# Small unused gaps between the large on-chip arrays of a two-layer decoder trunk

## The chip, the cores and the metric

The kernel runs on one core of a Trainium2 chip. The metric is the device time of one execution in microseconds (us); the median of several executions is compared. One core has five engines that run their own instruction streams and wait for one another by semaphores: TensorE (PE, matrix products), VectorE (DVE), ScalarE (ACT), GpSimd (POOL) and SyncE (SP). The profile shows the loads of TensorE's stationary operand as an engine of its own (PEld). Arrays lie in the on-chip memory SBUF, which has 128 partitions; an address below is the byte offset in a partition, the same for all of them.

## The reference

A batch of one sequence of 256 positions and width 2048 goes through two layers, all in float32:

```python
h = x
for layer in range(2):
    hn = rms_norm(h, norm_mix[layer])
    if layer % 2 == 0:
        mix = recurrent_mixers(hn, ...)     # one projection 2048 -> 6144, RG-LRU and HGRN2 heads, 2048 -> 2048
    else:
        mix = dilated_attention(hn, positions, w_qkv, w_o)   # 16 heads, 2048 -> 6144, 2048 -> 2048
    h = h + mix
    h = h + squared_relu_mlp(rms_norm(h, norm_mlp[layer]), mlp_w1[layer], mlp_w2[layer])  # 2048 -> 8192 -> 2048
return rms_norm(h, final_norm)
```

Nearly all of the work is in the seven large weight matrices.

## The kernel before

**Products in parts.** A float32 product is made of float32r matmuls (a type that TensorE takes at one column per step, with fewer bits). Each weight tile `raw` of 128 x 2048 is split into `hi` (ScalarE, a cast, L112) and `lo` = raw - hi (VectorE, L113). The activations are split likewise into a high and a low half that lie beside each other in `bufa` and `bufb` (16 blocks of 2 x 256 columns each). Of the four partial products three are computed: high x hi, high x lo, low x hi.

**Two forms.** In `direct` (L230), used by the input projections of layer 0, the weight part is the stationary operand (128 columns of `hi` or `lo`) and 256 columns of `bufa` or `bufb` are streamed. In `tokens` and in `times` inside `blocks`, used everywhere else, an activation slice of 128 columns is stationary and 512 columns of `hi` or `lo` are streamed. Every matmul has another stationary operand than the one before it, or loads the same one anew, so one weight load stands between any two matmuls. They all go through the helper `mm` (L196), which also fixes their order on TensorE.

**Seven products for eight.** `blocks` multiplies 2 x 2 blocks with seven products. The sums of activation blocks that this needs are kept, split, in `formx` (in the pool `both`) and `formh` (in the pools `pair0`, `forms1`); they are stationary operands too. Sums of weight blocks are formed in `s` and `t`, by VectorE and by DMAs that add on their way, and split like `raw`.

**What sets the order.** The loads of weights (SP's queue, some on POOL's) are issued in the order of a list of units, a few units ahead of their use. A scheduler places the instructions on each engine by priorities; small pieces of other work (transposes, attention heads, normalizations) are put off by a counter and slipped in between groups of twelve large matmuls.

**Where the arrays lie.** Pools take their addresses one behind the other, in the order in which they are opened, and a tile's place follows from the sizes ahead of it, rounded up to 32 bytes. First come the constants (`cst`), then `act` with `xall` and `bufa`, then `wraw`, `whi`, `wlo` with three tiles of 8 KB each, `tmp` with small tiles, `acts` with `bufb`, and behind it either the pools of layer 0's mixers or `both`, `pair0` and their successors. All large tiles are multiples of 512 bytes. In the built program before, `bufa` starts at 23328, `raw` at 56096, `hi` at 80672, `lo` at 105248, `bufb` at 132384, `formx` at 165152 and `formh` at 197920: each is 288 modulo 512. Every slice that a matmul reads of them starts a multiple of 512 bytes further on (128 columns of 4 bytes, or 256, or 512). `qk` and `st`, small tiles of layer 0's HGRN2 heads, lie at 416 modulo 512.

Of the kernel before, what the change touches and what calls it, by code (L numbers as in the profile page):

```python
# [10 lines left out]
F32 = mybir.dt.float32  # L11
# [9 lines left out]
P = 128  # L21
# [21 lines left out]
def trunk_kernel(ctx, tc, begin, xtok, cols, tab, masks, pos, fin, w_in, w_gate, w_out, w_qkv, w_o, w1, w2, out):  # L43
# [3 lines left out]
    act = pool("act")  # L47
# [3 lines left out]
    tmp = pool("tmp", 2)  # L51
# [8 lines left out]
    xall = act.tile([P, KB * S], F32, name="xall")  # L60
    xres = xall.rearrange("p (j d) -> p j d", j=2)
    bufa = act.tile([P, KB, 2 * S], F32R, name="bufa")

    units = []
    made = {}
# [138 lines left out]
    def put_off(wait, *fs):  # L204
        later.extend((clock[0] + wait, f) for f in fs)
# [369 lines left out]
    pairs, turned_ = ExitStack(), ExitStack()  # L575

    def open_pairs(layer):
        pool_ = pairs.enter_context(tc.tile_pool(name=f"pair{layer}", bufs=1))
        return pool_, pool_.tile([P, 4, 2, 512], F32R, name="formh")

    def part_forms(f, k, m, at, src):
# [8 lines left out]
        V.tensor_tensor(s4, a12, s2, OP.add)  # L590

    both = ctx.enter_context(tc.tile_pool(name="both", bufs=1))
    formx = both.tile([P, 4, 2, 512], F32R, name="formx")
    pair, formh = open_pairs(0)


# [6 lines left out]
    late = []  # L603
# [48 lines left out]
    def pair_forms(forms, k, src, z):  # L652
        h, l = (src[:, k:k + 2, c * S:c * S + S].bitcast(F32) for c in range(2))
        V.tensor_tensor(z.rearrange("p i j c -> p i (j c)"), h, l, OP.add)
        a11, a21, a12, a22 = (z[:, i, j] for i in range(2) for j in range(2))
        combos(a22, a11, a21, a12, a11, a21, a12, a22)
        part_forms(forms, k % 8 // 2, 1, slice(0, 4), z.rearrange("p i j (one c) -> p one (i j) c", one=1))
# [260 lines left out]
    def token_pair(i, c0, ready, raw=()):  # L918
        spare_ = wk.tile([P, 512], F32, name="q0", bufs=1) if not c0 and ATTENTION[:i].count("q") % 2 else None

        def out_(n, j):
            return xres[:, j, c0 + 512 * n:c0 + 512 * n + 512] if spare_ is None or (n, j) != (0, 0) else spare_

        def put(n, j, r=rt):
            def event(bank):
                with urgent():
                    if (n, j) in raw:
                        A.copy(out_(n, j), bank)
                    else:
                        A.activation(out_(n, j), bank, AF.Copy, scale=r[:, j:j + 1])  # L930
            return event

        def add(n, j, bank, r=rt):
            o = out_(n, j)
            with urgent():
                if (n, j) in raw:
                    V.tensor_tensor(o, bank, o, OP.subtract)
                else:
                    V.scalar_tensor_tensor(o, bank, r[:, j:j + 1], o, op0=OP.mult, op1=OP.add)

        def whole(n, j):
            if (n, j) in raw:
                with urgent():
                    A.activation(out_(n, j), out_(n, j), AF.Copy, scale=rt[:, j:j + 1])
            ready(n, j, out_(n, j))

        def final(n, j, bank):
            if (n, j) != (1, 0):
                put(n, j)(bank)
            else:  # L950
                add(n, j, bank)
            if (n, j) != (1, 1):
                whole(n, j)

        def u3(bank):
            add(1, 1, bank, rtn)
            whole(1, 1)

        blocks(w_qkv, 8 * i, 0, feature, formx,
               {"t2": put(1, 0, rtn), "t3": u3}, final)  # L960

    def queries_keys(i, raw=()):
        turned = [wk.tile([P, 4, S], F32, name="qT", bufs=1), wk.tile([P, 4, S], F32, name="kT", bufs=1)]

        def ready(n, j, o):
            t = o.rearrange("p (h c) -> p h c", h=4)
            r = t[:, :, :32].rearrange("p h (two c) -> p h two c", two=2)
            per = lambda a: a[:, j][:, None, :].to_broadcast([P, 4, 16])
            with urgent():
                b = wk.tile([P, 4, 2, 16], F32, name="rb", bufs=2)  # L970
                c = wk.tile([P, 4, 2, 16], F32, name="rc", bufs=2)
                V.tensor_tensor(b[:, :, 0], r[:, :, 1], per(sinT[:, 0]), OP.mult)
                V.tensor_tensor(b[:, :, 1], r[:, :, 0], per(sinT[:, 1]), OP.mult)
                V.tensor_tensor(c, r, cosT[:, j][:, None, None, :].to_broadcast([P, 4, 2, 16]), OP.mult)
                V.tensor_tensor(r, c, b, OP.add)

            def turns():
                p = psc.tile([P, 4, P], F32, name="pl", bufs=2)
                for h in range(4):
                    turn(p[:, h], t[:, h])  # L980
                with urgent():
                    A.copy(turned[n][:, :, j * P:j * P + P], p)

            put_off(WAIT_Q, turns)

        token_pair(i, 0, ready, raw)
        return turned

    def head(hd, q, k, wait):
        def scores():  # L990
            ps_ = psc.tile([P, 384], F32, name="pl", bufs=2)
            mm(ps_[:, :P], q[:, :P], k[:, :P], start=True, stop=True)
            mm(ps_[:, P:], q[:, P:], k, start=True, stop=True)
            s = wk.tile([P, 384], F32, name="as", bufs=3)
            nm = wk.tile([P, 2], F32, name="nm", bufs=3)
            ll = wk.tile([P, 2], F32, name="ll", bufs=3)
            with urgent():
                for j, sl in enumerate((slice(0, P), slice(P, 384))):
                    V.tensor_tensor_reduce(s[:, sl], ps_[:, sl], lnc[:, sl], -P ** -0.5, 3e38, OP.add, OP.min,
                                           nm[:, j:j + 1])  # L1000
                    lut(s[:, sl], s[:, sl], AF.Exp, bias=nm[:, j:j + 1], scale=-1.0, accum_out=ll[:, j:j + 1])
                V.reciprocal(ll, ll)
                for j, sl in enumerate((slice(0, P), slice(P, 384))):
                    A.activation(s[:, sl], s[:, sl], AF.Copy, scale=ll[:, j:j + 1])
            put_off(wait, lambda: turned(s))

        def turned(s):
            pt = psc.tile([P, 384], F32, name="pd", bufs=1)
            for j in range(3):
                turn(pt[:, j * P:j * P + P], s[:, j * P:j * P + P])  # L1010
            st = wkt.tile([P, 384], F32, name="pT", bufs=8)
            with urgent():
                A.copy(st, pt)
            ready_[hd] = st

        return scores

    def mix(hd, st):
        vs = slice(D // 2 + (hd % 8) * P, D // 2 + (hd % 8) * P + P)
        po = psc.tile([P, S], F32, name="pd" if hd % 2 else "po", bufs=1)  # L1020
        mm(po, xres[:, 0, vs], st[:, :S], start=True, stop=False, skip_group_check=True)
        mm(po[:, P:], xres[:, 1, vs], st[:, S:], start=False, stop=True, skip_group_check=True)
        z = tmp.tile([P, S], F32, name="z")
        with urgent():
            A.copy(z, po)
        split_to(mixed(hd), z)
# [3 lines left out]
    for i, what in enumerate(ATTENTION):  # L1030
        if what == "v":
            token_pair(i, D // 2, lambda *_: None)
            if hd == 16:
                assert len(ready_) == 8
                mixers.close()
                late.append(pairs.enter_context(tc.tile_pool(name="forms1", bufs=1)).tile(
                    [P, 8, 512], F32R, name="formh"))
            put_off(2, *(lambda h=h: mix(h, ready_.pop(h)) for h in range(hd - 8, hd)))
            if hd == 8:
                put_off(EARLY, *(lambda k=k: pair_forms(early_forms, k, bufb, wk.tile(  # L1040
                    [P, 512], F32, name="q0", bufs=1).rearrange("p (i j c) -> p i j c", i=2, j=2))
                    for k in range(0, 8, 2)))
        else:
            q, k = queries_keys(i, ((1, 0),) if not i else ())
            for h in range(4):
                put_off(WAIT_Q + 1 + 2 * h, head(hd, q[:, h], k[:, h], WAIT_S))
                hd += 1
# [141 lines left out]
```

## Time and profile before

| what | value |
|---|---|
| median of 3 runs | 2132.87 us (2132.70 to 2132.93) |
| profiled execution | 2133.06 us, span of the instructions 2131.3 us |
| granted TensorE clock, mean | 0.999 |
| busy share of the span | TensorE 100%, weight loads 84%, VectorE 84%, ScalarE 65%, GpSimd 3% |
| data moved by DMA | 488.71 MB, 229 GB/s mean |

A row of the chain in order of time has the start in us, the length in us, the engine, the tile written, the line of the kernel and the number of instructions. A row of the timeline has the start, the time from the first start to the last end, the engine, line and operation, the output and the inputs (streamed operand first, stationary second) with shapes, and how many equal instructions follow each other. Matmuls are pipelined: an end lies behind the next one's start, so the distance between starts is what counts. In the rows of groups stand the busy time, the mean of one in ns, and the idle time ahead of them with what ended it.

### The profile page before, as it was taken

What the parts mean: (1) busy time and instruction counts of PE and PEld (TensorE: products, weight loads), DVE (VectorE), ACT (ScalarE), POOL (GpSimd) and SP (SyncE); (2) the same over time, 40 slices, a digit from 0 to 9 for tenths busy, and PEclk for the clock granted to TensorE, in tenths of its full rate; (3) what the DMA queues carried; (4) which work ended last, traced back from release to release, by engine and by line L of the source; (5) the groups of instructions that cost most, each with busy time, mean ns of one, the idle gap of its engine ahead of it and who ended that gap; (6) DMA issues with size and microseconds to landing.
All of it is one profiled execution on the core that took longest, in us unless ns stands there. A gap on an engine that the chain in (4) does not pass through costs nothing.

```text
span 2131.3 us, 26730 instructions
## 1 busy us (share of the span) xinstructions
PE 2120.9 (100%) x10542; PEld 1797.6 (84%) x10542; DVE 1788.8 (84%) x1962; ACT 1378.2 (65%) x1543; POOL 66.8 (3%) x85
## 2 busy tenths in 40 slices
PE   9999999999999999999999999999999999999998
PEld 8989998888888888888888888888888888888886
DVE  7777888888888888888988797788897888888887
ACT  7445565776476567567666777776756765755764
POOL 0000000000000000000000000000000000000000
PEclk9999999999999999999999999999999999999999
DMA  8444446686777677677887767777767768777773
GB/s 336 162 162 158 161 148 224 206 269 233 227 237 253 230 240 253 227 241 231 270 279 218 241 199 247 254 247 228 246 237 253 236 212 269 238 234 227 271 225 146
DMA packets 69806, 488.71 MB, mean 229 GB/s; under 512 B 7808, under 2 KB 8320, under 8 KB 11952
## 3 DMA queue, kind: packets, MB, share of 16 engines
q1 hardware_dynamic: 58176, 410.96, 51.1%
q0 software_dynamic: 11216, 75.70, 18.3%
q8 instruction: 82, 1.34, 0.3%
q14 instruction: 44, 0.36, 0.0%
q10 hardware_dynamic: 288, 0.34, 0.0%
HBM read 482.78 MB, written 4.19 MB: 228 GB/s over the span
## 4 chain that ended last, share of the span: by engine, by line
PE 99%; DVE 0%; ACT 0%; DMA 0%; issue 0%; ACTq 0%; DVEq 0%; POOLq 0%
PE p L196 62%; PE po L196 14%; PE pd L196 13%; PE pt L196 5%; PE pl L199 2%; PE pl L470 1%; PE pl L196 0%; PE pd L199 0%; DMA ppi<-in_pos 0%; PE pd L454 0%; DVE lo L113 0%; ACT hi L112 0%; PE pl L465 0%; PE po L495 0%; PE po L496 0%
## 5 line engine op out<-in xcount | busy, mean ns | idle before, releaser
L113 DVE TENSOR_TENSOR lo<-raw,hi 128x2048 fp32r<-128x2048 f32 (+2 forms) x397 | 787.1, 1991 | 164.5 <-ACT hi L112 159.4
L112 ACT CAST hi<-raw 128x2048 fp32r<-128x2048 f32 (+2 forms) x397 | 657.3, 1671 | 335.1 <-PE p L196 175.5
L196 PE MATMUL p<-hi,bufa 128*128 128x512 f32 x1488 | 482.0, 394 | 0.0
L196 PE MATMUL p<-hi,bufb 128*128 128x512 f32 x1128 | 363.1, 391 | 0.0
L196 PEld LDWEIGHTS p<-hi,bufa 128*128 128x128 f32 x1488 | 279.2, 188 | 57.3 <-DVE bufa L245 0.5
L113 DVE TENSOR_TENSOR lo<-s,hi 128x2048 fp32r<-128x2048 f32 (+1 forms) x164 | 285.9, 1753 | 28.6 <-ACT hi L112 27.6
L112 ACT CAST hi<-s 128x2048 fp32r<-128x2048 f32 (+1 forms) x164 | 242.7, 1480 | 98.2 <-DVE s L164 54.2
L196 PE MATMUL p<-lo,bufa 128*128 128x512 f32 x744 | 287.6, 390 | 0.2 <-DVE lo L113 0.2
L196 PEld LDWEIGHTS p<-hi,bufb 128*128 128x128 f32 x1128 | 211.7, 188 | 43.7
L196 PE MATMUL p<-lo,bufb 128*128 128x512 f32 x564 | 219.5, 389 | 0.0
L196 PE MATMUL p<-bufa,hi 128*128 128x256 f32 x1024 | 193.2, 287 | 0.0
L196 PEld LDWEIGHTS p<-lo,bufa 128*128 128x128 f32 x744 | 139.9, 188 | 28.0 <-DVE lo L113 0.7
L196 PEld LDWEIGHTS p<-bufa,hi 128*128 128x128 f32 x1024 | 161.2, 191 | 0.2
L196 PE MATMUL p<-bufa,lo 128*128 128x256 f32 x512 | 146.5, 286 | 0.0
L112 ACT CAST hi<-t 128x2048 fp32r<-128x2048 f32 x41 | 78.5, 1914 | 99.6 <-PE p L196 91.1
L113 DVE TENSOR_TENSOR lo<-t,hi 128x2048 fp32r<-128x2048 f32 x41 | 94.0, 2292 | 55.4 <-ACT hi L112 55.0
L196 PEld LDWEIGHTS p<-lo,bufb 128*128 128x128 f32 x564 | 105.9, 188 | 21.5
L196 PE MATMUL p<-hi,formh 128*128 128x512 f32 x368 | 120.7, 391 | 0.0
L196 PE MATMUL p<-hi,formx 128*128 128x512 f32 x352 | 115.9, 390 | 0.0
L196 PE MATMUL po<-hi,bufb 128*128 128x512 f32 x320 | 103.7, 390 | 0.0
L196 PEld LDWEIGHTS p<-bufa,lo 128*128 128x128 f32 x512 | 98.0, 191 | 0.0
L164 DVE TENSOR_TENSOR s<-s,raw 128x1024 f32<-128x1024 f32 x82 | 96.4, 1216 | 0.1
(319 smaller groups left out, 3292.4 us busy)
## 6 DMA issues: line engine op xcount, KB each, us to landing
raw<-in_w SPq DMA_DIRECT2D x224, 1024.0 KB, 6.1
raw<-in_w_in SPq DMA_DIRECT2D x44, 1024.0 KB, 4.8
raw<-in_w_qkv SPq DMA_DIRECT2D x42, 1024.0 KB, 6.9
t<-in_w SPq DMA_DIRECT2D x32, 1024.0 KB, 4.9
t<-in_w POOLq DMA_DIRECT2D x32, 1024.0 KB, 8.7
s<-in_w POOLq DMA_DIRECT2D x17, 1024.0 KB, 8.4
raw<-in_w_out SPq DMA_DIRECT2D x15, 1024.0 KB, 4.8
raw<-in_w_o SPq DMA_DIRECT2D x14, 1024.0 KB, 7.7
```

The source lines that it names most:

```text
L112: a = A.copy(h, w)
L113: v = V.tensor_tensor(l, w, h.bitcast(F32), OP.subtract)
L164: V.tensor_tensor(s, s, held["c"][:, at:at + 1024], OP.add)
L196: chain[:] = [after(T.matmul(*args, **kw), chain)]
L199: chain[:] = [after(T.transpose(out_, in_, ident), chain)]
L470: T.matmul(pl[:, j], kq[:, js], halves(qp[:, js], c, True), start=True, stop=True)
```

## The change

Five tiles are allocated that nothing reads or writes. They lie at the end of `act`, in `tmp`, and at the start of `both`, `pair0` and `forms1`, and push what follows by 64 or 128 bytes.

```diff
     bufa = act.tile([P, KB, 2 * S], F32R, name="bufa")
+    act.tile([P, 16], F32, name="gap0", bufs=1)
+    tmp.tile([P, 32], F32, name="gap1", bufs=1)
...
     def open_pairs(layer):
         pool_ = pairs.enter_context(tc.tile_pool(name=f"pair{layer}", bufs=1))
+        pool_.tile([P, 16], F32, name="gap3", bufs=1)
         return pool_, pool_.tile([P, 4, 2, 512], F32R, name="formh")
...
     both = ctx.enter_context(tc.tile_pool(name="both", bufs=1))
+    both.tile([P, 16], F32, name="gap2", bufs=1)
     formx = both.tile([P, 4, 2, 512], F32R, name="formx")
...
-                late.append(pairs.enter_context(tc.tile_pool(name="forms1", bufs=1)).tile(
+                forms1 = pairs.enter_context(tc.tile_pool(name="forms1", bufs=1))
+                forms1.tile([P, 16], F32, name="gap4", bufs=1)
+                late.append(forms1.tile(
                     [P, 8, 512], F32R, name="formh"))
```

In the built program the offsets modulo 512 become:

| array | before | after |
|---|---|---|
| `bufa` | 288 | 288 |
| `raw`, `hi`, `lo` | 288 | 352 |
| `bufb` | 288 | 480 |
| `formx` | 288 | 32 |
| `t`, `s` | 288 | 32 |
| `formh` (both pools) | 288 | 96 |
| `qk`, `st` | 416 | 96 |

## The prediction

> **What bounds the kernel now.** I read the page's first two parts, then the chain of work, then that chain in order of time, and last the timeline of single matmuls, since the change can only touch what one instruction costs.
>
> ```profile
> span 2131.3 us, 26730 instructions
> PE 2120.9 (100%) x10542; PEld 1797.6 (84%) x10542; DVE 1788.8 (84%) x1962; ACT 1378.2 (65%) x1543; POOL 66.8 (3%) x85
> PEclk9999999999999999999999999999999999999999
> ...
> PE 99%; DVE 0%; ACT 0%; DMA 0%; issue 0%; ACTq 0%; DVEq 0%; POOLq 0%
> ```
>
> TensorE is busy for the whole span at the full granted clock, and 99% of the chain that ends last is TensorE. So the time is a sum over matmuls of the distance from one start to the next. That distance is steady. The chain in order of time (start, length, what):
>
> ```profile
> 217.18 6.72 PE p L196 x56
> 592.87 13.60 PE p L196 x60
> ```
>
> The first row is a run of 256-column float32r matmuls in the input projections: 6.72 / 56 = 120.0 ns each. The other is a run of 512-column ones: 13.60 / 60 = 226.7 ns each. 256 more columns cost 106.7 ns, so one column costs 0.417 ns and each matmul pays a further 13.3 ns whatever its width (226.7 - 512 x 0.417). The built program has 7,956 float32r matmuls of 512 columns and 1,632 of 256: 7,956 x 0.2267 = 1,803 us and 1,632 x 0.120 = 196 us, together 1,999 of the 2,131.3 us.
>
> What does the stationary operand do meanwhile? From the timeline of an MLP stretch (start, duration, engine):
>
> ```profile
> 1000.05 0.39 PE L196 MATMUL po<-lo,bufa 128*128 128x512 f32 x1
> ...
> 1000.73 0.39 PE L196 MATMUL po<-lo,bufa 128*128 128x512 f32 x1
> 1000.73 0.41 PEld L196 LDWEIGHTS po<-hi,bufa 128*128 128x128 f32 x2
> ```
>
> The next weight load starts in the same 10 ns in which a matmul starts (both 1000.73). So while 512 columns of one array are streamed, 128 columns of another are read, from the same instant on, at a fixed distance in addresses. That distance is all that the change alters.
>
> **The change, part by part.** It adds five small tiles and nothing that uses them. No instruction, DMA or wait is added, removed or moved: the two built programs hold the same instructions, access patterns and waits in the same order on every engine, and only base addresses differ. No queue is passed by anything, and no buffer comes free earlier or later by the program's order. The gaps take 320 bytes of a partition beside the tiles, which still fit.
>
> *Addresses.* Before, raw, hi, lo, bufa, bufb, formx and formh all start at 288 modulo 512, and every slice that a matmul reads starts a multiple of 512 bytes further on: stationary minus moving is 0 in all 9,588 cases. After, the offsets are hi and lo 352, bufa 288, bufb 480, formx 32, formh 96. Counted in the program, the distances become -64 for bufa under hi and lo (3,288 matmuls), +128 for bufb (2,604), +192 for formx (1,056), +256 for formh (1,008), and 64 in size for nearly all 256-column ones.
>
> *What a displaced pair costs.* The trace has no float32r pair at another distance, so I bound it by rows. After a short burst of other matmuls, the float32r stream does not return to 226.7 ns at once:
>
> ```profile
> 150.67 0.39 PE L470 MATMUL pl<-qk 128*128 128x64 f32 x2
> 150.87 0.47 PE L196 MATMUL p<-lo,bufa 128*128 128x512 f32 x1
> 151.18 0.63 PE L196 MATMUL p<-hi,bufa 128*128 128x512 f32 x2
> 151.64 0.40 PE L196 MATMUL p<-lo,bufa 128*128 128x512 f32 x1
> 151.88 0.62 PE L196 MATMUL p<-hi,bufa 128*128 128x512 f32 x2
> 152.34 0.40 PE L196 MATMUL p<-lo,bufa 128*128 128x512 f32 x1
> 152.57 0.62 PE L196 MATMUL p<-hi,bufa 128*128 128x512 f32 x2
> 153.03 0.39 PE L196 MATMUL p<-lo,bufa 128*128 128x512 f32 x1
> 153.26 0.62 PE L196 MATMUL p<-hi,bufa 128*128 128x512 f32 x2
> 153.72 0.39 PE L196 MATMUL p<-lo,bufa 128*128 128x512 f32 x1
> 153.94 0.62 PE L196 MATMUL p<-hi,bufa 128*128 128x512 f32 x2
> 154.40 0.39 PE L196 MATMUL p<-lo,bufa 128*128 128x512 f32 x1
> 154.62 0.62 PE L196 MATMUL p<-hi,bufa 128*128 128x512 f32 x2
> ```
>
> From 151.18 to 153.26 are nine matmuls, 2.08 / 9 = 231.1 ns each; from 153.26 to 154.62 six, 1.36 / 6 = 226.7 ns. No idle time of TensorE is shown in this stretch. So 226.7 ns is a state into which the two reads settle, and out of it a matmul costs 4.4 ns more on average. The slowest pair that I found in such a stretch:
>
> ```profile
> 127.69 0.63 PE L196 MATMUL p<-hi,bufa 128*128 128x512 f32 x2
> 128.16 0.39 PE L196 MATMUL p<-lo,bufa 128*128 128x512 f32 x1
> ```
>
> 0.47 / 2 = 235 ns, 8.3 ns above the settled state. That end gives 7,956 x 8.3 ns = +66 us. The other end, below nothing, is what another kind of matmul pays beside its columns, a transpose of 128 columns in plain float32:
>
> ```profile
> 620.08 0.87 PE pl L199 x8
> ```
>
> That is 0.87 / 8 = 108.8 ns. If each column takes two steps of 0.417 ns there, 128 columns are 106.7 ns and 2.1 ns are left over, an estimate. If float32r paid 2.1 in place of 13.3 ns, 9,588 x 11.2 ns = 107 us would go.
>
> I take +4.4 ns for each of the 7,956, by the nine-matmul row: the settled state was reached with all distances at 0, the same instructions out of it are the nearest thing to a displaced pair, and I have no row that tells the four distances apart. 7,956 x 4.4 ns = 35 us. I take nothing for the 256-column ones, because in their stretches a displaced read already occurs and changes nothing:
>
> ```profile
> 112.23 0.28 PE L196 MATMUL p<-bufa,lo 128*128 128x256 f32 x1
> 112.36 0.28 PE L196 MATMUL p<-bufa,hi 128*128 128x256 f32 x1
> 112.48 0.55 PE L470 MATMUL pl<-qk 128*128 128x64 f32 x4
> ```
>
> Here bufa (288) is streamed at 112.36 while the load of qk (416, so 128 apart) goes on, and the next start comes 0.12 us later, as between equal offsets. Its bounds are 10 ns either way by the rounding of these starts, 1,632 x 10 ns = 16 us.
>
> *The other engines.* VectorE and ScalarE read the same arrays at new offsets, but raw, hi and lo move together.
>
> ```profile
> L113 DVE TENSOR_TENSOR lo<-raw,hi 128x2048 fp32r<-128x2048 f32 (+2 forms) x397 | 787.1, 1991 | 164.5 <-ACT hi L112 159.4
> L113 DVE TENSOR_TENSOR lo<-t,hi 128x2048 fp32r<-128x2048 f32 x41 | 94.0, 2292 | 55.4 <-ACT hi L112 55.0
> ```
>
> The splits of t change their distance (t at 32, hi at 352). I cost them at nothing: VectorE has 16% of the span free, and the last column shows it waiting for ScalarE. Were that cover gone, each 10 ns on its 1,962 instructions would be 20 us. The DMAs write the same bytes to addresses moved by multiples of 64; the queue that carries SP's transfers takes 51% of the engines' time, so they stay hidden under TensorE, and a slower TensorE gives them more room.
>
> ```profile
> q1 hardware_dynamic: 58176, 410.96, 51.1%
> ```
>
> **The sum.** The profiled execution took 2133.06 us (span 2131.3 and 1.8 around it), 0.19 above the median of 2132.87. 2133.06 + 35 = 2168 us.
>
> **Rivals.** *Same.* 13.3 ns is a fixed price of a float32r matmul and the unsettled stretches come from the preceding burst, not from addresses; or the reads settle again at 226.7 ns at the new distances. For it: 512-column rows with bufa, bufb, formx and formh all run at 226.7 ns, and every unsettled stretch ends there. Against it: these rows never differ in distance. 2133 us. The Trainium skill, "SBUF — State Buffer", section "Who interferes with whom", gives TensorE two independent read ports, one for the moving operand and one for weight loads, and says that it never waits on anyone. By that rule the change does nothing. The 231.1 ns stretch agrees with it only if its cause is elsewhere, which no run here shows.
>
> *Faster.* The two reads collide because their offsets are equal, and the 13.3 ns are those collisions. It decides where a displaced distance brings the distance between starts below 226.7 ns. Complete, it gives 2133 - 107 = 2026 us; if it holds at the distance of bufb alone, 2,604 x 11.2 ns = 29 us and 2104 us. For it: plain float32 matmuls pay 2.1 ns, and the weight load runs from the same instant. Against it: the row at 112.36, where a distance of 128 saved nothing. The Trainium skill, "TensorE: Matmul & The Clock Gate", section "Wait — 56ns, not 53.3ns?", gives columns / 2.4 GHz + about 2.5 ns for a warm matmul; by that page 512 columns would be 215.8 ns, an estimate that no float32r row here reaches.
>
> *Much slower.* The new distances cost the 8.3 ns of the slowest pair: 2133 + 66 = 2199 us.
>
> **How the numbers follow.** Within 0.2% (4.3 us) is about what a measurement of this kernel can't tell from no change. Slower by more: 0.55 (of it 0.07 beyond 2200 us); same 0.22; faster 0.23 (of it 0.11 below 2105 us). The likeliest is the slow case, 2168 us; its own range is 2145 to 2199. The range for 8 in 10 takes in the same case and the mild end of the fast one: 2105 to 2200.
>
> **What would show it.** Right: the 60-matmul pieces of the chain grow from 13.60 to some 13.87 us while the 56-matmul piece stays at 6.72, counts on all engines stay, waits of TensorE for hi and lo shrink. The distances may show apart: rows with bufb, formx, formh and bufa each with their own pace. Same is shown by 13.60 in all of them; fast by pieces nearer 12.9. The prediction would be wrong where the settled state does not depend on the distance, or where a particular distance is better than 0. The first test is then which array's rows moved.

## The result, and the profile after

The changed kernel takes 2150.85 us (median of 3 runs, 2150.83 to 2151.46) against 2132.87 us: 18.0 us more, a ratio of 1.0085 with a 95% interval of 1.0063 to 1.0108. It is slower, as forecast, by half of the 35 us. The profiled execution took 2150.85 us with a span of 2149.1, so 17.8 us of span are to be explained.

The page of the changed kernel, its first two parts and the shares of the chain:

```profile
span 2149.1 us, 26730 instructions
PE 2137.8 (99%) x10542; PEld 1793.2 (83%) x10542; DVE 1789.1 (83%) x1962; ACT 1378.6 (64%) x1543; POOL 66.8 (3%) x85
PEclk9999999999999999999999999999999999999999
...
PE 98%; DVE 1%; ACT 1%; DMA 0%; issue 0%; ACTq 0%; POOLq 0%
```

The counts are those of before on every engine, VectorE and ScalarE work as long as before (1789.1 and 1378.6 against 1788.8 and 1378.2 us), the clock is full, and TensorE alone has grown, from 2120.9 to 2137.8 us. So each matmul is to be looked at. The chain in order of time (start, length, what) of the changed kernel:

```profile
214.68 6.60 PE p L198 x56
221.67 4.94 PE p L198 x43
...
353.61 16.73 PE p L198 x72
...
592.20 13.73 PE p L198 x60
...
2123.66 8.37 PE p L198 x36
```

and those of before that answer to the second, third and last of these rows:

```profile
224.28 5.21 PE p L196 x43
...
357.84 16.33 PE p L196 x72
...
2106.27 8.16 PE p L196 x36
```

The first two rows are runs of 256-column matmuls: 117.9 ns each where 120.0 stood, and 114.9 in place of 121.2. They became *faster*, and by unequal amounts. The runs of 72 and 36 have slices of `bufb` as stationary operand: 16.73 - 16.33 = 0.40 us over 72 is 5.6 ns each, 0.21 over 36 is 5.8 ns. The piece of 60, four fifths of it with `bufa` and the rest with `formx`, grew by 0.13 us, 2.2 ns each. That the 36 belong to `bufb` is read in the timeline of the changed kernel (start, duration, engine, output and inputs, streamed operand first):

```profile
2123.49 0.40 PE L198 MATMUL p<-hi,bufb 128*128 128x512 f32 x1
...
2131.63 0.40 PE L198 MATMUL p<-hi,bufb 128*128 128x512 f32 x1
2131.87 0.40 PE L198 MATMUL po<-hi,bufb 128*128 128x512 f32 x1
```

From the first to the third row are 36 matmuls, 8.38 / 36 = 232.8 ns each. TensorE has no idle time in this stretch.

To close the account I took from the trace every distance from one start of a float32r matmul to the next and grouped them by width and array. The means leave out the few distances above 260 (or 140) ns, where other work lies in between; the differences hold them too. A distance counts for the array of the later of the two matmuls:

| columns, array (distance, modulo 256) | number | before, ns | after, ns | difference, us |
|---|---|---|---|---|
| 512, `bufa` (-64, that is 192) | 3,203 | 227.4 | 229.2 | +5.9 |
| 512, `bufb` (128) | 2,580 | 226.9 | 232.6 | +14.4 |
| 512, `formx` (192) | 1,042 | 227.0 | 229.0 | +2.0 |
| 512, `formh` (0) | 1,000 | 227.0 | 228.1 | +1.1 |
| 256, `bufa` (64) | 1,469 | 119.8 | 115.8 | -5.6 |

"Distance" is, as in the prediction, the offset of the stationary operand less that of the moving one. The sum is +17.8 us, the whole growth of the span; the matmuls that these five rows leave out changed by less than 1 us.

### The profile page after: what moved, and what is told of

It reads as the page before. It is cut to its first block, busy times and chain, and to the rows that moved or that the text cites. A ratio compares the mean times of both kernels' runs of the same rounds, so it can differ in the third digit from the quotient of the medians.

```text
span 2149.1 us, 26730 instructions
## 1 busy us (share of the span) xinstructions
PE 2137.8 (99%) x10542; PEld 1793.2 (83%) x10542; DVE 1789.1 (83%) x1962; ACT 1378.6 (64%) x1543; POOL 66.8 (3%) x85
## 4 chain that ended last, share of the span: by engine, by line
PE 98%; DVE 1%; ACT 1%; DMA 0%; issue 0%; ACTq 0%; POOLq 0%
PE p L198 62%; PE po L198 14%; PE pd L198 13%; PE pt L198 5%; PE pl L201 2%; PE pl L472 1%; PE pl L198 0%; PE pd L201 0%; DMA ppi<-in_pos 0%; PE pd L456 0%; DVE lo L115 0%; ACT hi L114 0%; ACT L227 0%; DVE xc L549 0%; ACT gi L227 0%
## 5 line engine op out<-in xcount | busy, mean ns | idle before, releaser
L115 DVE TENSOR_TENSOR lo<-raw,hi 128x2048 fp32r<-128x2048 f32 (+2 forms) x397 | 787.0, 1991 | 176.5 <-ACT hi L114 173.3
L198 PE MATMUL p<-hi,bufb 128*128 128x512 f32 x1128 | 369.4, 396 | 0.0
L198 PE MATMUL p<-bufa,hi 128*128 128x256 f32 x1024 | 187.5, 283 | 0.0
L115 DVE TENSOR_TENSOR lo<-t,hi 128x2048 fp32r<-128x2048 f32 x41 | 94.0, 2292 | 58.5 <-ACT hi L114 57.4
```

The costliest lines, as they stand in the source:

```text
L115: v = V.tensor_tensor(l, w, h.bitcast(F32), OP.subtract)
L198: chain[:] = [after(T.matmul(*args, **kw), chain)]
```

## The experiments

### The distance alone, with all else idle

The first question is whether the addresses act on TensorE's own two reads, or on those reads against the traffic of the other engines and the DMAs. `distances`, the first of three such runs and called the bench below, is a kernel that holds nothing but streams of 72 float32r matmuls, one after another, each with its own offsets:

```diff
+CASES = [(0, d) for d in MOVED] + [(64, 64), (128, 128), (192, 192), (64, 0), (128, 0), (0, 0)]
...
+    at = s // 4 + (4 * r + i) % 16 * 512 + a * 256          # 512 columns: s moves the stationary slice, m the streamed one
+    todo.append((st[:, at:at + P], mv[b][:, m // 4 + i * 512:m // 4 + i * 512 + 512]))
...
+    T.matmul(p[:, :width], x, y, start=k == 0, stop=k == len(todo) - 1)
```

> This kernel leaves the whole computation out: it only streams float32r matmuls, 72 for each case, from arrays whose offsets are chosen (m is the offset added to the streamed operand, s to the stationary one), 26 cases with 512 and 26 with 256 columns, while the other engines stand still. Distance theory (the pace is set by stationary minus moving modulo 512): 512 columns take 226.7 ns at distance 0, some 232.5 at 128, 229 at 192 and 448, 228 at 256; 256 columns take 120.0 at 0 and some 116 at 64; the cases moved together (64/64, 128/128, 192/192) are as 0/0, and 64/0 as 0/448. Offset theory (where an array itself starts decides): the cases moved together differ from 0/0 by 1 to 6 ns. Traffic theory (displaced arrays collide with what VectorE, ScalarE and the DMAs access): with nothing else running, 226.7 and 120.0 ns in all cases.

Its chain in order of time; the tile's name holds the width, the bytes m by which the moving operand is shifted, and s by which the stationary one is:

```profile
81.90 17.08 PE w512m0s64x L53 x72
...
117.56 17.00 PE w512m0s128x L53 x72
...
153.08 16.77 PE w512m0s192x L53 x72
...
188.34 16.65 PE w512m0s256x L53 x72
...
294.69 16.77 PE w512m0s448x L53 x72
...
382.35 16.63 PE w512m128s128x L53 x72
...
452.27 16.60 PE again512m0s0x L53 x72
...
507.16 8.76 PE w256m0s64x L53 x72
...
544.41 8.44 PE w256m0s192x L53 x72
...
702.11 8.90 PE again256m0s0x L53 x72
```

Each 0.07 us in these rows is 1 ns for each matmul. At equal offsets 72 matmuls of 512 columns take 16.60 us, 128 apart 17.00, 64 apart 17.08. Moved together by 128 they take 16.63, and 256 apart 16.65, as if they were equal. The steady distances (from the starts of the last two thirds of each stream, since the first matmuls have not settled) are:

| distance, bytes | 512 columns, ns | 256 columns, ns |
|---|---|---|
| 0 | 226.7 | 120.0 |
| 16 | 226.7 | 118.3 |
| 32 | 233.3 | 118.3 |
| 64 (and 320) | 233.3 | 117.8 |
| 96 (and 352) | 234.2 | 117.4 at 96, 118.6 at 352 |
| 128 (and 384) | 232.4 | 118.7 at 128, 120.0 at 384 |
| 192 (and 448) | 228.9 | 113.3 |
| 224 (and 480) | 233.3 | 116.7 |
| 256 | 226.7 | 120.0 |
| 496 | 226.7 | 117.4 |

Behind the start of the first stream no other engine works during them, and the DMA share is 0.00, so traffic is not needed for the price. For 512 columns the distance decides, and it repeats every 256 bytes (for 256 columns not in every pair of rows). The kernel pays what the streams pay: 192 costs 228.9 here and 229.2 (`bufa`) and 229.0 (`formx`) there, 128 costs 232.4 here and 232.6 (`bufb`) there. Only the 256-column matmuls, at 64, differ: 117.8 here, 115.8 on average there. (The 16 bytes of the second row were measured right behind the stream at distance 0 alone, which matters further down.)

### All arrays moved together

```diff
+    act.tile([P, 16], F32, name="gap", bufs=1)      # ahead of xall: every large array moves by 64 bytes
     xall = act.tile([P, KB * S], F32, name="xall")
```

> A 64-byte gap ahead of xall moves all large arrays by 64, so that every distance stays 0 and every absolute offset changes from 288 to 352. Distance theory: 2133 us, 512 columns at 226.7 ns. Offset theory: hi and lo at 352 as in the changed kernel, so up to its +18 us, 2151. Traffic theory: 2133, since all arrays keep their places to one another.

2132.78 us, a ratio of 1.0000 (0.9990 to 1.0009). Its chain shows the numbers of before, 13.60 and 16.34 us:

```profile
357.57 16.34 PE p L197 x72
...
592.50 13.60 PE p L197 x60
```

So it is not the new offsets that cost, but that they differ.

### One gap at a time

`act_gap` has only the gap behind `bufa`. `bufa` then lies 64 bytes before all the others, which stay together.

```diff
     bufa = act.tile([P, KB, 2 * S], F32R, name="bufa")
+    act.tile([P, 16], F32, name="gap0", bufs=1)
```

> Only gap0: bufa stays at 288 and all other large arrays lie at 352, so only pairs with bufa are displaced, by 64. Distance theory: bufa's 512-column matmuls +1.8 ns (+5.9 us), the 256-column ones -4.0 ns (-5.6 us), the others unchanged: 2133 us. Offset theory: bufb, formx and formh pay as their new offset of 352 asks, so they leave 226.7 ns.

2134.78 us, a ratio of 1.0010 (1.0000 to 1.0019). Two parts of the change nearly cancel here: the 512-column matmuls with `bufa` cost 4.9 us more (229.1 ns), the 256-column ones 5.4 us less (115.9 ns). `formx`, at distance 0 but next to the displaced `bufa`, costs 0.8 us more. `bufb`, whose distance is 0 too, stays near its old pace (16.36 us for the 72):

```profile
221.23 4.94 PE p L197 x43
...
352.86 16.36 PE p L197 x72
```

`tmp_gap` has only the gap in `tmp`. `bufb`, `formx` and `formh` then all lie 128 bytes further on than `hi` and `lo` (modulo 512), and `bufa` lies with them.

```diff
+    tmp.tile([P, 32], F32, name="gap1", bufs=1)
```

> Only gap1: bufb, formx and formh lie at 416, the rest at 288, so all three are at +128 to hi and lo. Distance theory: formx and formh take bufb's 232.5 ns too, 4,622 matmuls x 5.6 ns = +26 us, 2159 us. Theory that each array has its own price: bufb 232.5, formx 229.0, formh 228.1 as in the changed kernel, +17.5 us, 2150.

2159.23 us, a ratio of 1.0125 (1.0110 to 1.0140): one tile of 128 bytes costs 26 us, more than all five together.

```profile
358.75 16.73 PE p L197 x72
...
597.91 13.73 PE p L197 x60
```

`bufb` pays what it pays in the changed kernel (16.73 us, +14.1 us in all), `formx` +6.0 and `formh` +5.3 us, at 232.3 to 232.8 ns. `bufa` at distance 0 pays +1.9 us: the piece of 60 contains 47 matmuls with `bufa` at 227.7 ns and 13, nearly all with `formx`, at 232.8. A displaced stream leaves the next one out of its settled state for some matmuls, even where that one has equal offsets. That is also where the +1.1 us of `formh` in the changed kernel can come from, which the next run tests.

### The period of 256 bytes, in the kernel

```diff
+    tmp.tile([P, 64], F32, name="gap1", bufs=1)     # 256 bytes in place of 128
```

> Only a gap in tmp, of 256 bytes: bufb, formx and formh stand 256 from hi and lo. Theory of a 256-byte period: as distance 0, 2133 us, 512 columns at 226.7 to 227.0 ns. Theory of a 512-byte period, in which formh's +1.1 ns in the changed kernel is the price of 256: 4,622 matmuls x 1.1 ns = +5 us, 2138 us.

2133.03 us, a ratio of 1.0001 (0.9992 to 1.0010).

```profile
357.86 16.33 PE p L197 x72
...
592.89 13.60 PE p L197 x60
```

256 bytes cost nothing. In the changed kernel `formh` lies 256 bytes from `hi` (modulo 512), so its own distance is free, and its +1.1 us must come from what runs around it. The trace agrees: 0.8 us of it lie in the first four `formh` matmuls behind another array and 0.3 us in the next four, and from the ninth on they take 226.6 to 227.0 ns in both kernels.

### Bytes inside a line

`distances_2` repeats the streams with steps that are no multiple of 16, and with both operands moved by 4 or 8 bytes.

```diff
-MOVED = (0, 16, 32, 48, 64, 96, 128, 160, 192, 224, 256, 288, 320, 352, 384, 416, 448, 464, 480, 496)
-CASES = [(0, d) for d in MOVED] + [(64, 64), (128, 128), (192, 192), (64, 0), (128, 0), (0, 0)]
+MOVED = (0, 4, 8, 12, 20, 80, 112, 144, 176, 184, 188, 196, 200, 208, 216, 232, 240, 244, 248, 252)
+CASES = [(0, d) for d in MOVED] + [(4, 4), (8, 8), (8, 0), (4, 196), (8, 200), (0, 0)]
```

> As the run called distances (the whole computation left out, matmul streams alone), with finer steps: distances that are no multiple of 16 bytes, steps between 128 and 256, and both operands moved by 4 or 8. Theory of a 256-byte period in 16-byte lines: 226.7 ns for 512 columns within 16 bytes of distance 0 and more elsewhere; for 256 columns the lowest, 113.3 ns, near 192, and 120.0 at 0; operands moved together as 0/0. If single bytes count, the steps of 4 and 8 differ from their neighbours at multiples of 16.

The chain in order of time:

```profile
28.89 17.01 PE w512m0s4x L53 x72
...
294.75 16.63 PE w512m0s240x L53 x72
...
365.49 17.39 PE w512m4s4x L53 x72
383.59 17.07 PE w512m8s8x L53 x72
...
437.19 17.44 PE w512m8s200x L53 x72
455.34 16.63 PE again512m0s0x L53 x72
```

No distance gives fewer than 226.7 ns with 512 columns; 240 (that is -16) gives just that. And at distance 0 it matters where both begin: 4 bytes off, 237.8 ns; 8 bytes off, 233.1. The worst is 240.0 ns with the moving operand 8 bytes off and the stationary one at 200. The Trainium skill, "SBUF — State Buffer", section "Specifications (TRN2)", says that this memory has lines of 16 bytes and that each crossing to a new line pays a penalty. The price of the 4 and 8 bytes agrees with such lines; the page gives no size for it.

### Two views of one array

For 256 columns a displaced pair is faster, for 512 slower, and `bufa` serves both. In `two_views` it lies 64 bytes further on than the others (modulo 512) in layer 0, where the 256-column matmuls are, and with them afterwards.

```diff
-    bufa = act.tile([P, KB, 2 * S], F32R, name="bufa")
+    both_views = act.tile([P, KB * 2 * S + 16], F32R, name="bufa")
+    bufa = both_views[:, 16:].rearrange("p (k c) -> p k c", k=KB)
+    act.tile([P, 112], F32, name="gap", bufs=1)
...
     mixers.close()                                   # end of layer 0's mixers
+    bufa = both_views[:, :KB * 2 * S].rearrange("p (k c) -> p k c", k=KB)
```

> All arrays at distance 0, but bufa is read and written 64 bytes further on during layer 0 (its tile is longer by 64 bytes, and a gap fills it up to 512), so that there hi and lo stand at -64 to the streamed bufa, and bufa at +64 to the streamed hi and lo. Distance theory with the prices of the first run: 256 columns 113.3 in place of 119.8 ns, 1,469 x 6.4 ns = -9.4 us; 370 matmuls of 512 columns at 233.3 ns, +2.4 us: 2126 us, faster than the kernel before and the changed one. Were the prices those of single arrays, 2133 to 2135.

2131.89 us, a ratio of 0.9995 (0.9986 to 1.0004): a miss.

```profile
223.78 5.12 PE p L198 x43
```

The 256-column matmuls took 117.7 ns on average and not 113.3: -2.9 us in place of -9.4. The cost beside it came out as expected, +2.5 us for the 512-column ones of layer 0.

`two_views_back` turns the sign round: `bufa` at the old place in layer 0, `hi` and `lo` 64 bytes further on, which is the distance of the changed kernel and of `act_gap`, and 0 afterwards.

```diff
+    both_views = act.tile([P, KB * 2 * S + 16], F32R, name="bufa")
+    bufa = both_views[:, :KB * 2 * S].rearrange("p (k c) -> p k c", k=KB)
...
     mixers.close()
+    bufa = both_views[:, 16:].rearrange("p (k c) -> p k c", k=KB)
```

> bufa lies at offset 0 in layer 0 and 64 bytes further on after it, hi and lo 64 bytes after the old place throughout. So the 1,536 matmuls of 256 columns have their stationary hi or lo 64 bytes past the moving bufa (the distance of the changed kernel and of act_gap, where they took 115.8 and 115.9 ns in place of 119.8), some 384 matmuls of 512 columns of layer 0 have bufa 64 bytes before hi and lo, and the other 2,900 with bufa, and all with bufb, formx and formh, lie at distance 0. Theory (only the distance of the two operands decides): 256 columns -5.4 us, 384 matmuls of 512 columns by 1.7 to 2.5 ns = +0.6 to +1.0 us, all else 0: 2128 to 2129 us, faster than both kernels, ratio 0.998. Rival (the gain of 256 columns in act_gap hangs on the whole layout, not on this distance): no gain, 2133 to 2134 us.

2129.01 us, a ratio of 0.9981 (0.9972 to 0.9991): faster than both kernels.

```profile
221.61 4.94 PE p L197 x43
...
588.33 13.60 PE p L197 x60
```

The 256-column pieces have the pace of the changed kernel (4.94 us for 43; 116.3 ns on average, -4.8 us), and the later 512-column ones that of before (13.60). The matmuls of 512 columns with `bufa` cost +0.6 us.

### Broken streams

Why did 113.3 ns not come in `two_views`? In layer 0 the 256-column stream is interrupted by other work, mostly every 7 to 56 matmuls. `distances_3` breaks its streams too:

```diff
+CASES = [(d, n) for n in (72, 24, 8) for d in (0, 64, 128, 192, 448)] + [(0, 72)]
...
+    if k % n == n - 1 and k < len(todo) - 1:
+        for u in range(4):
+            T.matmul(q, raw[:, u * P:u * P + P], raw[:, 512:576], ...)
```

> The computation is left out: streams of 72 matmuls at distances 0, 64, 128, 192 and 448, unbroken, and broken after every 24 and after every 8 by four plain float32 matmuls of 64 columns, as the 256-column matmuls of layer 0 are broken in the kernel. If breaks are why two_views took 117.7 ns at 448 and not the 113.3 of the unbroken stream, and why act_gap took 115.9 at 64 and not 117.8: the steady distances of 256 columns in the broken streams come to some 116 to 118 ns at 448 and some 116 ns at 64, and stay 120.0 at distance 0. If breaks have no part in it: 113.3 at 448 and 192 and 117.8 at 64 in the broken streams too. For 512 columns breaks at most pull the pace towards 226.7 ns: with breaks 128 costs less than the 232.4 ns of the unbroken stream, without a part of theirs the same.

In its chain the name ends with the matmuls between two breaks:

```profile
20.28 8.76 PE w256s64n72x L54 x72
...
48.13 8.76 PE w256s448n72x L54 x72
...
61.37 2.93 PE w256s0n24x L54 x24
...
72.66 2.88 PE w256s64n24x L54 x24
...
106.67 2.88 PE w256s448n24x L54 x24
```

Neither explanation holds as I put it. At 448 even the unbroken stream takes 117.8 ns here, where `distances` had 113.3 (8.44 us at 544.41 above for 192, the same for 448). So a 256-column stream at one distance has more than one steady pace. At 64, breaks after every 24 give 116.3 ns on average in place of 117.8, but no piece has that pace: the three run at 113.3, 117.7 and 117.8. The kernels show the same two paces. In each, 46 unbroken stretches of 256-column matmuls with `bufa` are 14 or more long; from their ninth matmul on they take:

| kernel, distance | 113.2 to 113.4 ns | 117.6 to 118.0 ns |
|---|---|---|
| `act_gap`, 64 | 21 stretches | 25 stretches |
| changed, 64 | 19 | 27 |
| `two_views_back`, 64 | 21 | 25 |
| `two_views`, 448 | 1 | 45 |

None lies between, and in the kernel before all 46 take 119.8 to 120.0 ns. So the 115.8 ns of the changed kernel are a mean of two paces, the rows of 4.94 and 6.60 us above show one of each, and `two_views` missed because nearly all of its stretches took the slower pace, of which its forecast knew nothing. What selects the pace was not found. It isn't the chip: `act_gap` and `two_views_back` ran on two different ones and show the same counts. Nor does the kind of the interruption alone decide: in `act_gap`, behind the same four matmuls of 64 columns, some stretches take 113.3 ns and others 117.8.

The 512-column streams showed the same steady paces broken after 24 as unbroken, 233.4 at 64, 232.3 at 128, 228.9 at 192. Broken after every 8, the stream at distance 0 has no time to settle: over the last five distances of each piece it takes 231.7 ns on average, more than the 229.2 at 192.

### One line of 16 bytes

If 16 bytes either way are free for 512 columns and a gain for 256, one constant offset would do without a second view.

```diff
-    bufa = act.tile([P, KB, 2 * S], F32R, name="bufa")
+    wide = act.tile([P, KB * 2 * S + 128], F32R, name="bufa")
+    bufa = wide[:, 4:KB * 2 * S + 4].rearrange("p (k c) -> p k c", k=KB)     # plus_16; minus_16: from 124
```

> bufa alone lies 16 bytes further on, for the whole kernel, and nothing else moves modulo 512. Its 3,288 matmuls of 512 columns then have the stationary operand 16 bytes past the moving one, where the bench showed 226.7 ns as at distance 0; its 1,536 of 256 columns have it 16 bytes before (240 modulo 256), where the benches showed 117.4. Theory (the distance modulo 256 decides in the kernel as in the bench): 512 columns 0, 256 columns 1,469 steady ones x 2.4 ns = -3.5 us: about 2129.3 us, by one constant offset. Rival (in the kernel, with its breaks and its changes of array, a displacement by one line costs the 512-column matmuls too, as most others do): with 1 to 2 ns on 3,288 of them 2133 to 2136 us.

2136.86 us, a ratio of 1.0020 (1.0011 to 1.0028): slower, a miss of the theory as it stood.

> bufa alone lies 16 bytes before the old place. 512 columns at distance -16 (240 modulo 256): 226.7 ns in the bench, so 0. 256 columns at +16: 118.3 ns in the bench, so 1,469 x 1.5 ns = -2.2 us: about 2130.7 us by the theory. Rival as in plus_16: 2133 to 2136 us.

2130.51 us, a ratio of 0.9989 (0.9980 to 0.9998): as the theory had it, though the interval barely leaves out no change. The chain of `plus_16` shows why the two differ:

```profile
156.50 6.35 PE p L197 x27
...
591.91 13.60 PE p L197 x60
```

The long piece, which begins inside a longer stream, runs at the settled 226.7 ns, as the bench said. But the piece of 27, right behind a burst of other matmuls, takes 6.35 us, 235.2 ns each; in the kernel before it is

```profile
156.77 6.23 PE p L196 x27
```

230.7 ns, and 6.20 us in `minus_16`. Sorted by how many 512-column matmuls have run since the last interruption, those with `bufa` take on average:

| since the break | before, ns | `plus_16`, ns | `minus_16`, ns | after, ns |
|---|---|---|---|---|
| 0 to 7 | 230.0 | 232.2 | 229.1 | 230.1 |
| 8 to 15 | 227.3 | 232.0 | 227.6 | 229.1 |
| 16 to 23 | 226.7 | 232.3 | 227.8 | 228.8 |
| 24 to 31 | 226.8 | 230.4 | 227.5 | 228.9 |
| 32 to 39 | 226.7 | 228.8 | 227.2 | 229.2 |
| 64 and more | 226.7 | 227.2 | 226.8 | 229.0 |

Before, a stream settles within some 16 matmuls. The column of `plus_16` looks like a slower settling, over some 40, but its means hide two steady paces. Taken one by one, from the ninth matmul on, its 75 stretches of 16 or more matmuls with `bufa` run at 226.7 ns (44 of them) or at 232.5 to 233.5 (31), and the first of the program keeps 233.3 for 142 matmuls, to its end. Of the 35 stretches behind an interruption 30 have the slow pace. The 40 behind another array, which is at distance 0, all begin with the fast one, and only one leaves it: it goes from 226.7 to 233.3 ns behind a wait of TensorE of 0.2 us. The timeline of `plus_16` shows the change:

```profile
622.62 0.40 PE L197 MATMUL pd<-hi,bufa 128*128 128x512 f32 x1
...
625.42 0.40 PE L197 MATMUL po<-hi,bufa 128*128 128x512 f32 x1
...
630.96 0.39 PE L197 MATMUL po<-hi,formx 128*128 128x512 f32 x1
...
633.68 0.39 PE L197 MATMUL p<-hi,bufa 128*128 128x512 f32 x1
...
636.40 1.04 PE L200 MATMUL pl<-tab__199,y 128*128 128x128 f32 x8
```

The 12 matmuls from 622.62 on, with `bufa`, take 233.3 ns each, the 12 with `formx` from 630.96 on 226.7, and the 12 with `bufa` behind them, from 633.68 on, 226.7 as well. At +16 a stream thus keeps the pace that it has until it is interrupted, and a stream at distance 0 directly ahead of it brings the fast one. In this kernel, with its many interruptions, that costs 5.5 us. At -16 the two paces are 226.7 and 228.2 to 228.5 ns (49 and 26 of 75 stretches), and the whole costs nothing (-0.5 us); at 192, in the changed kernel, 74 of 75 stretches stay near 229. Why some interruptions lead to the slow pace and others don't was not found, nor why the bench showed the fast one alone. The 256-column matmuls gained in both, 2.7 us in `plus_16` (117.8 ns) and 3.6 us in `minus_16` (117.2 ns).

## Why the prediction was right, and where it was not

**TensorE bounds, and the matmul's distance is the whole sum: right.** The five groups of float32r matmuls account for 17.8 us of 17.8.

**Instructions, order and other engines unchanged: right; the waits nearly.** The counts are equal, and the splits of `t`, whose distance changed, cost the same 2292 ns. The groups of VectorE in the changed kernel:

```profile
L115 DVE TENSOR_TENSOR lo<-raw,hi 128x2048 fp32r<-128x2048 f32 (+2 forms) x397 | 787.0, 1991 | 176.5 <-ACT hi L114 173.3
L115 DVE TENSOR_TENSOR lo<-t,hi 128x2048 fp32r<-128x2048 f32 x41 | 94.0, 2292 | 58.5 <-ACT hi L114 57.4
```

Their idle time grew (164.5 to 176.5 us for `raw`), as work beside a slower TensorE does. That TensorE's waits for `hi` and `lo` would shrink was empty: there was one of 0.2 us before, and there is one of 0.2 us now. All of TensorE's waits together went from 1.7 to 2.5 us, by one of 0.6 us for `bufa` and one of 0.4 us for `qk`.

**+4.4 ns for every 512-column matmul, 35 us: the sign right, the size too large.** The four arrays paid +1.8, +5.6, +2.0 and +1.1 ns. Their 23.4 us over 7,956 matmuls are 2.9 ns each. The prediction had no row that told the four distances apart and gave all one price; only `bufb`'s 128 costs more than that price, and `formh`'s 256 is free of itself. This term was 11.6 us too large. That the row it came from was so near is in part luck. Its 231.1 ns are a stream at distance 0 on its way to 226.7, while the displaced streams keep steady paces of their own, 228.9 at 192 and 232.4 at 128. And the sum came out at half of the 35 us only by the way in which the four distances fell: with 128 bytes for three of the arrays, `tmp_gap` pays 26 us.

**256-column matmuls at no price: wrong in size, and in a direction that its bounds of 16 us had kept open.** They gained 4.0 ns, 5.6 us in all. The step rested on one pair of starts at 112.36, rounded to 10 ns, with a distance of 128. There the bench has 118.7 for 120.0 ns, which such a row can't show. With it falls the fixed price of 13.3 ns "whatever its width": it was worked out from two rows, both at distance 0. 35.0 - 11.6 - 5.6 = 17.8 us is the result.

**The bounds.** The upper one, 8.3 ns for every matmul, was not reached at any distance that is a multiple of 16 bytes (at most 234.2 ns, 7.5 above). Off the line it is exceeded: 240.0 ns, 13.3 above.

**The rival "same".** Its first half, that 13.3 ns are fixed and the reads settle at any distance, fell with the first table of the bench: most distances keep a slower pace to the end of the stream. The rule beside it, of the Trainium skill, "SBUF — State Buffer", section "Who interferes with whom", by which TensorE's two read ports are independent and it waits for no one, does not give the time here: with every other engine idle, two streams that differ in nothing but the distance of their operands take 226.7 and 233.3 ns. That the two reads collide is the plain reading of this, but no run shows the ports themselves, and the mechanism stays open.

**The rival "faster".** It was right about the 256-column matmuls and about nothing else: at 49 pairs of offsets none brought 512 columns below 226.6 ns. By the Trainium skill, "TensorE: Matmul & The Clock Gate", section "Wait — 56ns, not 53.3ns?", a warm matmul pays about 2.5 ns beside its columns. No run here reached that: at 0.417 ns for a column, the least that a float32r matmul paid here, with a load for each, was 13.3 ns with 512 columns and 113.3 - 106.7 = 6.7 ns with 256.

## What to carry to other kernels

Where TensorE is the bound and every matmul loads a new stationary operand, look at both operands' offsets modulo 256 bytes: for 512 float32r columns in streams of some 16 matmuls and more keep them equal and on 16-byte lines, and after any new tile, however small and unused, check that they still are (one of 128 bytes cost 26 us here). A narrower stream may want another distance (here 64 bytes with 256 columns, 0.2% of the time), and the price must be measured in the kernel, with its interruptions, as well as in a bench: at some distances a stream has two paces, and what ran ahead of it picks one. A sum of "no change" can hide two effects, as in the kernel with one gap, +4.9 and -5.4 us; group the starts by array before believing it. A mean can hide two paces, too: look at the stretches one by one.

## What the runs showed of the hardware that I had not expected

- In the bench the pace of a 512-column float32r stream repeats with the distance of its operands every 256 bytes: 226.7 ns at 0, 16, 240 and 256, 228.9 at 192, 232 to 234 at most others.
- Bytes inside a 16-byte line count as well, even with equal offsets: 237.8 ns at 4 and 4, 233.1 at 8 and 8, up to 240.0.
- A displaced 256-column stream is faster, 113.3 to 118.7 ns in most cases against 120.0. At 64 and at 448 it has two steady paces, 113.3 and 117.8, and keeps one of them until it is interrupted.
- 512-column streams show the same in the kernel: 226.7 or 233.3 ns at +16, held for up to 142 matmuls, and 226.7 or 228.3 at -16. What ran ahead picks the pace: at +16 all 40 stretches directly behind a stream at distance 0 began with the fast one, and 30 of 35 behind an interruption had the slow one.
- A displaced stream unsettles the next one, even where that one has equal offsets: +1.9 us for `bufa` beside displaced neighbours, +1.1 us for `formh`.
